# Moving small work of a two-layer encoder between VectorE, ScalarE and Pool, with warm-up matmuls and latent units spread wider

## The chip, the cores and the metric

The kernel runs on one core of one Trainium2 chip. A core has TensorE (PE) with its weight loads (PEld), VectorE (DVE), ScalarE (ACT), GpSimd (POOL) and SyncE (SP), which starts the transfers. Each engine works off its own list of instructions in the order in which the program wrote them, and waits on semaphores of the others. The metric is the time on the device in microseconds, the median of three runs. Beside it stands one execution that the hardware profiler recorded, from which all durations come.

## The reference

`x` has 512 tokens of 1024 numbers in float32, and there are two layers:

```python
for l in range(DEPTH):
    h = rms_norm(x, attn_norm_g[l])
    c_q, c_kv, k_rope, gq, gk, gv, pool_in, gate_logits = split_columns(h @ w_in[l], IN_SIZES)
    o_mla = mla_branch(c_q, c_kv, k_rope, ...)     # low-rank q and kv, 8 heads, norms of heads, rope
    o_gqa = gqa_branch(gq, gk, gv, ...)            # 8 query heads, 2 key heads, norms of heads, rope
    o_pool = pool_branch(pool_in, ...)             # centred means over 2/4/8/16 tokens, minus the token
    gates = sigmoid(gate_logits)                   # three gates of 1024 columns
    merged = sum(gates[:, :, i] * (o_i @ w_branch_i) for the three branches)
    x = x + merged @ w_out[l]
    u = depthwise_conv(rms_norm(x, ffn_norm_g[l]) @ ffn_w_up[l], ...)
    x = x + (silu(u_gate) * u_val) @ ffn_w_down[l]
```

An RMS norm multiplies a row by the inverse root of its mean square. Such inverse roots are needed for the rows before both halves of a layer, for the two latents, and for the heads of queries and keys.

## The kernel before, in words

**Products.** TensorE's numbers are rounded float32 (fp32r). To keep the accuracy, every operand is cut in two, a high part (a copy that rounds) and a low part (the rest), and a product is three matmuls (`mm3`, lines 347 to 351): high by high, high by low, low by high. The weights are cut on the chip too: `w_split` (line 301) lets ScalarE copy the high part `wh` and VectorE or Pool subtract it, which gives `wl`. Four buffers of each go round, two pieces ahead of their use. Which engine subtracts is chosen by `pick` when the program is built, after the first eight pieces of the first layer, which are VectorE's.

**Order.** The program is written by a planner that runs while the kernel is built. `Clock` keeps a modelled time; `chain` starts each step of a chain of small operations when the step before would be done, `at` starts one at a given delay, `need` and `done` keep keys that a step waits for, and `Engine` books a modelled cost for every operation. The order in which the operations fall in this model is the order of each engine's list. So a change of one operation or of its booked cost can move others. No modelled time is read in this document.

**Stages of a layer.**

1. The latents: `tok_major` multiplies token blocks of `HH`/`HL` (high and low part of `x` times its gain) with eight pieces of 384 columns, into banks acc and ST. In the first layer `norm_steps` (line 382) makes `HH` on ScalarE, `HL` on VectorE, the squares `sqt` in turn on VectorE and ScalarE, and their sum `sq` on Pool, while the eight blocks of `x` arrive.
2. `norm_finish` (line 428): TensorE sums `sq` over the partitions, `rsqrt_steps` (line 405) takes the inverse root `rt` of 8 columns in ten operations on VectorE (a first guess from the bits and three Newton steps), then `dgh` and `dgl` are set up from it, from which TensorE and ScalarE make `rbc`, the root along the other axis (`norm_rows`, line 451).
3. Four groups of pool columns, `feat_major`, 24 matmuls each, into banks AV, AV, mi and S. `pool_steps` (line 601) evacuates each as `pp`, adds shifted copies (`win`, one to four sums by group), scales the edges, subtracts the token, and cuts the result in two (`mxh`, `mxl`).
4. The latents are scaled with their root `ssc`, turned by TensorE and cut (`cth`, `ctl`).
5. Queries of the grouped attention: eight pieces of 512 into AV, AV, mi and ST, then squares (`gqs`), rope (`rp`, `gqr`) and scaling by the root `ssr` (`gq_norm`, line 712).
6. Keys and values: eight pieces of 288, and in the middle `pool_product` (line 724), which uses the query banks again. The key `gk` gets rope and root, is turned (`gk_turn`, line 780) and cut into `ka` and `kb`.
7. Two attentions of eight heads, with filler units between their steps: gate units (`gate`, 3 matmuls of 512), branch units (`branch`), and units of the second attention's queries, keys and values from the latents (`make_q`, `make_n`, `make_v`). `gates` (line 804) gives them out, one latent unit before each gate or branch unit as long as there are latent units. Gate, branch and latent units share the two acc banks. `attention` holds a table of fixed positions for its own steps among the filler.
8. The output projection, the up projection with its convolution, and the down projection, bound by TensorE alone; the next layer's `HH`, `HL` and `sq` are made beside the last one.

`tables` (line 515) multiplies the rope tables with the gains of the heads, `tabg` four times 128x256 and `tabm` four times 128x128, on VectorE, once in a layer.

In the profile most rows stand at the line of a helper: L208 is ScalarE's activation, L215 a tensor_tensor and L219 a scalar_tensor_tensor of VectorE or Pool, L223 a reduction, L227 a tensor_scalar, L340 the matmul, L344 the turn.

Of the kernel before, what the change touches and what calls it, by code (L numbers as in the profile page):

```python
# [187 lines left out]
class Engine:  # L188
# [20 lines left out]

    def _two(self, out):  # L210
        self._count(out, *((0.002145, 0.127) if self.kind == "Pool" else (0.00105, 0.07)))

    def tensor_tensor(self, out, *a):
        self._two(out)
        return self.eng.tensor_tensor(out, *a)  # L215
# [27 lines left out]
def trunk(ctx: ExitStack, tc: tile.TileContext, x, w, prm, gb, cst, out):  # L243
# [115 lines left out]
    ident = C[:, C_ID:C_ID + P]  # L359
    ones = cp.tile([P, P], F32R, tag="ones", name="ones")  # L360


# [18 lines left out]

    def norm_steps(gen, kc, g, sq, sqe=None):
        xk = XM[:, kc, :]
        hh, hl = HH[:, kc, :], HL[:, kc, :]
        t = sq if kc == 0 else slot("sqt")

        def hi():
            A.activation(hh, xk, AF.Copy, scale=g)
            if sqe is None:
                A.activation(t[:, :T], xk, AF.Square)  # L390

        def lo():
            V.scalar_tensor_tensor(hl, xk, g, f(hh), ALU.mult, ALU.subtract)
            done("H", gen, kc)

        def add():
            if sqe is not None:
                sqe.tensor_tensor(t[:, :T], xk, xk, ALU.mult)
            if kc > 0:
                G.tensor_tensor(sq[:, :T], sq[:, :T], t[:, :T], ALU.add)  # L400
            done("sq", gen, kc)

        return [hi, lo, add]

    def rsqrt_steps(a, n, key, eng=None):

        y = small("y0", [P, 64])[:, :n]
        t = small("yt", [P, 64])[:, :n]

        def newton(to):  # L410
            if eng:
                eng.tensor_tensor(t, y, a, ALU.mult)
                eng.tensor_tensor(t, t, y, ALU.mult)
# [12 lines left out]
        return [go, lambda: done(*key)]  # L426
# [47 lines left out]

    def rope_steps(dst, src, cs, sn, shape, half, eng2):

        hold = []

        def parts():
# [10 lines left out]
            if dst is not src:  # L490
                V.tensor_tensor(dst, src, cs, ALU.mult)

        def add():
            if dst is src:
                V.tensor_tensor(dst, src, cs, ALU.mult)
            V.tensor_tensor(dst, dst, hold[0], ALU.add)

        return [parts, add]

    def layer(l, sq, xsrc):  # L500
# [14 lines left out]
        def tables():  # L515
# [85 lines left out]
        def pool_steps(g, acc, tag):  # L601
# [13 lines left out]
            def window(step):  # L615
# [164 lines left out]
        def gk_turn():  # L780
# [4 lines left out]
            def hi():  # L785
                for j in range(2):
                    ka, kb = KAB[j]
                    js = slice(64 * j, 64 * j + 64)
                    A.activation(ka[0:64, :T], kT[js], AF.Copy)
                    A.activation(ka[64:128, :T], kT[js], AF.Copy)  # L790

            def lo():
# [5 lines left out]
                done("kab", l)  # L798
            chain(hi, lo)

# [3 lines left out]
        def gates(br, okey, odst, mode):  # L804
# [46 lines left out]

            extra = None
            for k, m in _order(br):
                if k in mla_make:
                    extra = mla_make[k](m)
                    continue
                work = branch(m) if k == "b" else gate(m)
                more = True
                while more:
                    if extra:  # L860
                        if next(extra, END) is END:
                            extra = None
                        yield
                    more = next(work, END) is not END
                    yield
# [26 lines left out]
        def q_out(g, b, acc):  # L892
            j = slot("mqs")

            def copies():
                copy(MQ[g][:, b].rearrange("p h f -> p (h f)"), acc[:, :384])

            def squares():
                A.activation(j[:, :384], acc[:, :384], AF.Square)
# [5 lines left out]

            chain(copies, squares, sums)

# [51 lines left out]
        def n_out(g, p, acc):  # L959
# [6 lines left out]
            def squares():  # L966
                A.activation(j[:, :T], acc, AF.Square)
# [5 lines left out]

            chain(copies, squares, sums)

# [412 lines left out]
    nc.scalar.dma_start(prms[0][:, :PRM_W0], prm[0][:, :PRM_W0])  # L1388
    warm = small("warm", [P, 1], bufs=1)
    V.memset(warm, 0.0)  # L1390
# [9 lines left out]
    for j in range(LA + 1):  # L1400
        at(4.05 + 1.27 * j, lambda j=j: w_ahead(j))
    for kc in range(KC):
# [139 lines left out]
```

## Time and profile before

| | |
|---|---|
| median of 3 runs (1677.89 to 1677.95) | 1677.89 us |
| the profiled execution | 1680.6 us |
| its span, first to last instruction | 1678.8 us |
| mean granted TensorE clock | 0.996 |
| VectorE, ScalarE, Pool busy | 57%, 46%, 53% |
| layer 0 up to the output projection, and layer 1 likewise | 0 to 372 us, 845 to 1202 us |

A row of the timeline gives the start and the length in us, the engine, the line, the operation, what it writes and reads, the shape, and in brackets how long the engine had been idle before it and which operation ended that. "x3" means three operations in a row, and the length is that from the first one's start to the last one's end. A row of the windows gives for a stretch the busy time and, in brackets, the number of instructions of PE, PEld, DVE, ACT and POOL, then the granted clock, the share of the transfer engines, and GB/s.

### The profile page before, as it was taken

The numbers are of one execution on the slowest core, as the hardware profiler recorded it, in microseconds if no ns is written. First come the engines' busy times: TensorE is split into PE (matmuls) and PEld (weight loads), VectorE is DVE, ScalarE is ACT, GpSimd is POOL, SyncE is SP. The second block draws the span as 40 slices with busy tenths as digits, with TensorE's granted clock in tenths as the row PEclk, the third lists the DMA queues.
The fourth block names the chain that finished last, engine by engine and source line by source line (L and its number), as shares of the span: only waits on it lengthen the run. The fifth ranks groups of instructions, "written<-read, shape, count | busy, mean of one in ns | idle before, by whom it ended". The sixth has DMA issues, their size and how long they took to land.

```text
span 1678.8 us, 20300 instructions
## 1 busy us (share of the span) xinstructions
PE 1650.0 (98%) x7360; PEld 1336.1 (80%) x7360; DVE 949.4 (57%) x1542; ACT 774.0 (46%) x1364; POOL 886.6 (53%) x746
## 2 busy tenths in 40 slices
PE   8989999999999999999999999999999999999999
PEld 7777777778888888888887877777788888888887
DVE  7777767753356667630157677677533666666100
ACT  5356755553444444432234577455534444444221
POOL 4432763444566666655544427643446666566543
PEclk9999999999999999999999999999999999999999
DMA  4221111113323333233232211111233222222331
GB/s 174 79 85 44 57 61 53 48 52 124 124 86 93 96 94 100 88 112 114 99 108 79 82 45 60 60 51 47 70 116 119 88 93 96 99 90 90 113 118 57
DMA packets 44596, 145.40 MB, mean 87 GB/s; under 512 B 5072, under 2 KB 6352, under 8 KB 44496
## 3 DMA queue, kind: packets, MB, share of 16 engines
q1 hardware_dynamic: 44352, 144.10, 26.0%
q8 instruction: 58, 0.95, 0.2%
q14 instruction: 42, 0.34, 0.1%
q10 hardware_dynamic: 144, 0.01, 0.0%
HBM read 139.90 MB, written 4.19 MB: 86 GB/s over the span
## 4 chain that ended last, share of the span: by engine, by line
PE 91%; issue 4%; DVE 2%; ACT 1%; POOL 1%; DMA 0%; SPq 0%; POOLq 0%; DVEq 0%; ACTq 0%
PE ps_acc L340 41%; PE ps_ST L340 23%; PE ps_AV L340 23%; PE ps_S L340 2%; PE ps_mi L340 1%; POOL wl L215 1%; PE ps_mi L344 1%; DMA XM<-x 0%; ACT qa L208 0%; ACT wh L208 0%; DVE vml L215 0%; DVE nm L223 0%; DVE gqr L215 0%; ACT ka L208 0%; DVE vmh L231 0%
## 5 line engine op out<-in xcount | busy, mean ns | idle before, releaser
L215 POOL TENSOR_TENSOR wl<-raw,wh 128x512 fp32r<-128x512 f32 (+1 forms) x514 | 679.8, 1332 | 659.2 <-ACT wh L208 548.1
L208 ACT ACTIVATE wh<-raw 128x512 fp32r<-128x512 f32 (+3 forms) x522 | 315.0, 610 | 193.0 <-PE ps_ST L340 92.6
L219 DVE SCALAR_TENSOR_TENSOR a<-u,prm,a 128x512 f32<-128x512 f32 x176 | 239.8, 1363 | 79.4 <-ACT a L208 76.0
L340 PE MATMUL ps_acc<-HH,wh 128*128 128x512 f32 x592 | 234.7, 396 | 3.2 <-DVE XM L219 3.0
L340 PE MATMUL ps_acc<-HH,wl 128*128 128x512 f32 x592 | 234.0, 395 | 1.2 <-POOL wl L215 1.2
L340 PE MATMUL ps_acc<-HL,wh 128*128 128x512 f32 x592 | 233.6, 395 | 0.0
L340 PEld LDWEIGHTS ps_acc<-HH,wh 128*128 128x128 f32 x592 | 111.5, 188 | 30.3 <-ACT wh L208 4.5
L340 PEld LDWEIGHTS ps_acc<-HH,wl 128*128 128x128 f32 x592 | 111.4, 188 | 28.5 <-POOL wl L215 2.1
L340 PEld LDWEIGHTS ps_acc<-HL,wh 128*128 128x128 f32 x592 | 111.5, 188 | 25.4
L208 ACT ACTIVATE ps_ST<-ps_ST 128x512 f32<-128x512 f32 x128 | 74.5, 582 | 120.7 <-PE ps_ST L340 120.2
L340 PE MATMUL ps_AV<-HH,wh 128*128 128x512 f32 x288 | 113.9, 396 | 0.0
L340 PE MATMUL ps_AV<-HL,wh 128*128 128x512 f32 x288 | 113.8, 395 | 0.0
L340 PE MATMUL ps_AV<-HH,wl 128*128 128x512 f32 x288 | 113.7, 395 | 0.0
L223 DVE TENSOR_REDUCE nm<-ps_S 128x1 fp32r<-128x512 f32 x128 | 87.5, 684 | 45.1 <-PE ps_S L340 44.3
L215 DVE TENSOR_TENSOR pl<-ps_ST,ph 128x512 fp32r<-128x512 f32 x128 | 87.2, 682 | 32.8 <-ACT ph L208 32.2
L215 POOL TENSOR_TENSOR al<-a,ah 128x512 fp32r<-128x512 f32 x44 | 58.3, 1326 | 84.8 <-ACT ah L208 56.6
L340 PE MATMUL ps_ST<-HH,wh 128*128 128x512 f32 x240 | 95.0, 396 | 0.0
L340 PE MATMUL ps_ST<-HL,wh 128*128 128x512 f32 x240 | 94.8, 395 | 0.0
L340 PE MATMUL ps_ST<-HH,wl 128*128 128x512 f32 x240 | 94.8, 395 | 0.0
L208 ACT ACTIVATE a<-u,prm 128x512 f32<-128x512 f32 x88 | 72.0, 818 | 31.8 <-DVE u L215 31.8
L208 ACT ACTIVATE ah<-a 128x512 fp32r<-128x512 f32 x44 | 27.8, 633 | 116.3 <-DVE u L239 110.8
L208 ACT ACTIVATE a<-a 128x512 f32<-128x512 f32 x44 | 27.9, 635 | 113.7 <-DVE u L239 113.7
(343 smaller groups left out, 3545.4 us busy)
## 6 DMA issues: line engine op xcount, KB each, us to landing
raw<-w SPq DMA_DIRECT2D x228, 512.0 KB, 3.4
raw<-w SPq DMA_DIRECT2D x13, 384.0 KB, 2.9
XM<-x SPq DMA_DIRECT2D x16, 256.0 KB, 3.8
raw<-w SPq DMA_DIRECT2D x6, 448.0 KB, 3.3
xsp<-XM SPq DMA_DIRECT2D x8, 256.0 KB, 2.0
XM<-xsp SPq DMA_DIRECT2D x8, 256.0 KB, 3.3
out<-XM SPq DMA_DIRECT2D x8, 256.0 KB, 2.3
raw<-w SPq DMA_DIRECT2D x4, 432.0 KB, 3.0
```

Source lines behind the costliest of these rows:

```text
L208: return self.eng.activation(out, in_, func, **k)
L215: return self.eng.tensor_tensor(out, *a)
L219: return self.eng.scalar_tensor_tensor(out, *a)
L223: return self.eng.tensor_reduce(out, in_, *a, **k)
L340: PE.matmul(o, lhsT=lhsT, rhs=rhs, start=start, stop=stop)
L344: PE.transpose(o, src, ident)
```

## The change

- Pool gets from VectorE: the tables of the ropes, the window sums of the two wider pool groups, the last sum of the query ropes, and the scaling of the queries by their root. VectorE gets from Pool: the seven sums of squares in the first layer's start.
- All squares at that start are made by ScalarE, later than the cuts of `x`.
- Inverse roots of 8 columns become one power with exponent -0.5 on Pool (two for the rows, one for the latents, one for the key heads, in each layer). Roots of 32 columns stay as they were.
- The second copies of the key's high part are made by VectorE from the first ones and no longer by ScalarE from PSUM; the low part is placed 1.2 us later in the planner's time.
- Copy and squares of a latent unit are issued together.
- A latent unit comes before every second gate or branch unit.
- 34 matmuls of 128x128 on a tile of ones run at the start, and their result is not used.

```diff
-        self._count(out, *((0.002145, 0.127) if self.kind == "Pool" else (0.00105, 0.07)))
+        self._count(out, *((0.14, 0.1) if ALU.pow in a else (0.002145, 0.127) if self.kind == "Pool" else (0.00105, 0.07)))
...
-            if sqe is not None:
-                sqe.tensor_tensor(t[:, :T], xk, xk, ALU.mult)
             if kc > 0:
                 G.tensor_tensor(sq[:, :T], sq[:, :T], t[:, :T], ALU.add)
...
     def rsqrt_steps(a, n, key, eng=None):
+        if n == 8:
+            return [lambda: G.tensor_tensor(a, a, bc(mhalf, [P, 8]), ALU.pow), lambda: done(*key)]
...
             if dst is not src:
-                V.tensor_tensor(dst, src, cs, ALU.mult)
+                eng2.tensor_tensor(dst, src, cs, ALU.mult)
...
-            V.tensor_tensor(dst, dst, hold[0], ALU.add)
+            (eng or eng2).tensor_tensor(dst, dst, hold[0], ALU.add)
...
-                    V.tensor_tensor(
+                    G.tensor_tensor(
                         tb[:, 256 * i:256 * i + 256].rearrange("p (b f) -> p b f", b=4),
...
-                V.tensor_tensor(
+                G.tensor_tensor(
                     tabm[:, 128 * n:128 * n + 128].rearrange("p (b f) -> p b f", b=4),
...
-            chain(([("w", KC - 1), ("H", G1, KC - 1), ("sq", G1, KC - 1)], tables), after=16.0)
+            chain(([("rt", G1)], tables), after=20.0)
...
-                V.tensor_tensor(nx[:, c0:c1], wins[-1][:, i0[0]:i0[1]], wins[-1][:, i1[0]:i1[1]], ALU.add)
+                (G if g >= 2 else V).tensor_tensor(nx[:, c0:c1], wins[-1][:, i0[0]:i0[1]], wins[-1][:, i1[0]:i1[1]],
+                                                   ALU.add)
...
-            parts, add = rope_steps(o, q, cs, sn, [P, 8, 64], 32, V)
+            parts, add = rope_steps(o, q, cs, sn, [P, 8, 64], 32, V, G)
...
-            V.tensor_tensor(o, o, bc(ssr[:, 8 * b:8 * b + 8].unsqueeze(2), [P, 8, 64]), ALU.mult)
+            G.tensor_tensor(o, o, bc(ssr[:, 8 * b:8 * b + 8].unsqueeze(2), [P, 8, 64]), ALU.mult)
...
-              *[([("gqr", l, b)], lambda b=b: gq_norm(b)) for b in range(4)])
+              *[([("gqr", l, b), ("gkn", l)], lambda b=b: gq_norm(b)) for b in range(4)])
...
-                    A.activation(ka[64:128, :T], kT[js], AF.Copy)
+                    V.tensor_copy(ka[64:128, :T], ka[0:64, :T])
...
-            chain(hi, lo)
+            chain(hi, lambda: at(1.2, lo))
...
-                    extra = mla_make[k](m)
+                    extra, tick = mla_make[k](m), 0
...
-                    if extra:
+                    if extra and tick % 2 == 0:
...
+                    tick += 1
...
-            chain(copies, squares, sums)
+            chain(copies, sums)
...
+    idle = ps("mi")
+    for _ in range(34):
+        PE.matmul(idle[:, :P], lhsT=ones, rhs=ones, start=True, stop=True)
+    free("mi")
...
+    def square(kc, t):
+        A.activation(t[:, :T], XM[:, kc, :], AF.Square)
+        done("sqt", kc)
+    def sum_up(kc, t):
+        if kc > 0:
+            V.tensor_tensor(sq[:, :T], sq[:, :T], t[:, :T], ALU.add)
+        done("sq", 0, kc)
...
-        chain(*norm_steps(0, kc, prms[0][:, PRM_AG + kc:PRM_AG + kc + 1], sq, None if kc % 2 else V),
-              after=3.4 + 1.27 * kc)
+        chain(*norm_steps(0, kc, prms[0][:, PRM_AG + kc:PRM_AG + kc + 1], None)[:2], after=3.4 + 1.27 * kc)
+        at(9.0 + 1.27 * kc, lambda kc=kc: square(kc, sqt[kc]))
+    chain(*[([("sqt", kc)], lambda kc=kc: sum_up(kc, sqt[kc])) for kc in range(KC)], after=11.0)
```

Only the query rope is given Pool for its last sum; the key rope keeps VectorE. The built lists show the moves: VectorE's loses 114 instructions (1544 to 1430), Pool's gains 41 (751 to 792), TensorE's gains 34, and SyncE's transfers keep their order. Pool's list in each layer has the eight tables between weight subtractions of the first stage, the seven window sums between the pieces 16 to 21 of the layer, the four rope sums between the pieces 27 to 31, and the four scalings after the key's root, between the pieces 37 to 40.

More of the change, by code (lines that the diff above doesn't have):

```diff
@@ L208, in activation, with _two @@
         return self.eng.activation(out, in_, func, **k)
-    def _two(self, out):
-        self._count(out, *((0.002145, 0.127) if self.kind == "Pool" else (0.00105, 0.07)))
+    def _two(self, out, *a):
+        self._count(out, *((0.14, 0.1) if ALU.pow in a else (0.002145, 0.127) if self.kind == "Pool" else (0.00105, 0.07)))
     def tensor_tensor(self, out, *a):
-        self._two(out)
+        self._two(out, *a)
         return self.eng.tensor_tensor(out, *a)
@@ L360, in trunk @@
     ones = cp.tile([P, P], F32R, tag="ones", name="ones")
+    mhalf = cp.tile([P, 1], F32, tag="mhalf", name="mhalf")
     MQ, MK = [[cp.tile([P, 4, 4, 96], F32, tag=f"{n}{g}", name=f"{n}{g}") for g in range(2)] for n in ("MQ", "MK")]
@@ L379, in split, with norm_steps @@
         return steps
-    def norm_steps(gen, kc, g, sq, sqe=None):
+    def norm_steps(gen, kc, g, sq):
         xk = XM[:, kc, :]
         hh, hl = HH[:, kc, :], HL[:, kc, :]
-        t = sq if kc == 0 else slot("sqt")
+        t = sq if kc == 0 or sq is None else slot("sqt")
         def hi():
             A.activation(hh, xk, AF.Copy, scale=g)
-            if sqe is None:
+            if sq is not None:
                 A.activation(t[:, :T], xk, AF.Square)
@@ L473, in bc, with rope_steps @@
         return ap.to_broadcast(shape)
-    def rope_steps(dst, src, cs, sn, shape, half, eng2):
+    def rope_steps(dst, src, cs, sn, shape, half, eng2, eng=None):
         hold = []
@@ L850, in branch @@
                     chain(product, add, *split(mh[:, :T], ml[:, :T], XM[:, m, :]), fin)
-            extra = None
+            extra, tick = None, 0
             for k, m in _order(br):
                 if k in mla_make:
-                    extra = mla_make[k](m)
+                    extra, tick = mla_make[k](m), 0
                     continue
@@ L896, in copies @@
                 copy(MQ[g][:, b].rearrange("p h f -> p (h f)"), acc[:, :384])
-            def squares():
                 A.activation(j[:, :384], acc[:, :384], AF.Square)
@@ L964, in copies @@
                 copy(MK[g][:, bs, :, 0:64], acc.rearrange("p (b h f) -> p b h f", b=2, h=4))
-            def squares():
                 A.activation(j[:, :T], acc, AF.Square)
@@ L972, in sums @@
                 done("ssn", l, g, p)
-            chain(copies, squares, sums)
+            chain(copies, sums)
         def k_norm(g):
@@ L1389, in trunk @@
     warm = small("warm", [P, 1], bufs=1)
+    V.memset(mhalf, -0.5)
     V.memset(warm, 0.0)
@@ L1401, in trunk @@
         at(4.05 + 1.27 * j, lambda j=j: w_ahead(j))
+    def square(kc, t):
[5 more added lines that the diff above has]
+        done("sq", 0, kc)
+    sqt = [sq] + [slot("sqt") for _ in range(1, KC)]
     for kc in range(KC):
-        chain(*norm_steps(0, kc, prms[0][:, PRM_AG + kc:PRM_AG + kc + 1], sq, None if kc % 2 else V),
-              after=3.4 + 1.27 * kc)
+        chain(*norm_steps(0, kc, prms[0][:, PRM_AG + kc:PRM_AG + kc + 1], None)[:2], after=3.4 + 1.27 * kc)
+        at(9.0 + 1.27 * kc, lambda kc=kc: square(kc, sqt[kc]))
+    chain(*[([("sqt", kc)], lambda kc=kc: sum_up(kc, sqt[kc])) for kc in range(KC)], after=11.0)
     at(30.0, lambda: V.tensor_copy(idr, ident))
```

## The prediction

> **What bounds the kernel now.** I read the engine table of the profile first, then the list of what TensorE waited for, then the granted clock in narrow windows, and last the order of each engine around every wait.
>
> ```profile
> PE 1650.0 (98%) x7360; PEld 1336.1 (80%) x7360; DVE 949.4 (57%) x1542; ACT 774.0 (46%) x1364; POOL 886.6 (53%) x746
> ```
>
> ```profile
> 372.71 63.19 PE ps_acc L340 x273
> ```
>
> TensorE is busy 98% of the span, and in the quiet parts (second row, from the chain that ended last) one 128x512 matmul starts every 63.19 / 273 = 0.231 us. No work is taken from TensorE here, so the change can only win what TensorE idles, or runs at a low clock. Both can be counted.
>
> ```profile
> PE ps_acc L340 <- ACT wh L208: 4.9, 1, 4.9
> PE ps_ST L340 <- DVE gqr L215: 4.1, 2, 2.0
> PE ps_acc L340 <- ACT mns L208: 3.0, 2, 1.5
> PE ps_acc L340 <- DVE XM L219: 3.0, 2, 2.1
> PE ps_acc L340 <- DVE wl L215: 2.0, 2, 1.8
> PE ps_acc L340 <- DVE vml L215: 1.8, 2, 0.9
> PE ps_AV L340 <- POOL wl L215: 1.7, 2, 0.9
> ...
> PE ps_acc L340 <- ACT mqs L208: 1.2, 2, 0.9
> PE ps_AV L340 <- ACT wh L208: 0.7, 1, 0.7
> ```
>
> These are TensorE's waits (total us, times, longest). The first is the wait for the first data; the other eight sum to 17.5 us.
>
> ```profile
> 14.16:17.58 3.42, 1.58 (x9) 1.25 (x8) 3.42 (x3) 1.06 (x3) 3.20 (x3) 1.00 0.90 360
> 17.58:20.99 3.41, 3.41 (x12) 3.41 (x12) 3.41 (x5) 0.53 (x1) 1.47 (x1) 0.50 0.44 178
> 21.00:24.41 3.41, 3.41 (x21) 3.41 (x21) 3.38 (x8) 0.64 (x1) 2.78 (x2) 1.00 0.00 0
> 61.95:65.36 3.41, 3.41 (x10) 2.67 (x9) 3.41 (x5) 0.00 (x0) 3.02 (x2) 0.50 0.31 83
> 116.56:119.98 3.42, 3.42 (x12) 2.80 (x10) 1.38 (x2) 2.23 (x5) 0.39 (x1) 0.50 0.46 153
> 918.69:922.10 3.41, 1.38 (x6) 0.82 (x5) 3.27 (x10) 1.64 (x3) 0.79 (x1) 1.00 0.00 0
> 922.10:925.52 3.42, 3.42 (x16) 3.41 (x15) 3.25 (x11) 1.27 (x3) 0.80 (x1) 0.50 0.14 16
> ```
>
> The second column is TensorE's busy time and, in brackets, its matmuls; after the five engines stands the granted clock. Four stretches of 3.41 us run at 0.50; the two whose predecessor is shown follow one in which TensorE was busy under half. At half clock 12 of the 384-column matmuls run instead of 21 (rows two and three): 9 x 0.175 = 1.6 us lost. At 61.95 it is 10 of the 512-column ones instead of 3.41 / 0.231 = 14.8, 1.1 us; the two mixed stretches I put at 1.4 each. So a wait of 2 us can cost 3.5.
>
> The Trainium skill, TensorE: Matmul & The Clock Gate, section "Why this matters for your kernels", asks for no idle gap over about 3 us. By that rule gaps of 2 us would leave the clock alone, and the sum below would be 5.5 us smaller, 1665. The trace does not agree, and so this has no chance of its own: 1.38 us busy in 3.41, a gap of about 2, was followed by 0.50.
>
> **The change part by part.**
>
> *Start of layer 0.* The squares leave VectorE for ScalarE, and the seven sums leave Pool for VectorE.
>
> ```profile
> 4.89 0.69 PE L340 MATMUL ps_acc<-wh,HH 128*128 128x384 f32 x1 [4.89 <-ACT wh L208]
> 12.01 7.06 POOL L215 TENSOR_TENSOR sq<-sq,sqt 128x512 f32<-128x512 f32 x4 [3.62 <-DVE sqt L215]
> 12.33 1.34 ACT L208 ACTIVATE wh<-raw 128x384 fp32r<-128x384 f32 x3
> 14.76 4.72 DVE L215 TENSOR_TENSOR wl<-raw,wh 128x384 fp32r<-128x384 f32 x3
> 28.43 0.95 PE L340 MATMUL ps_S<-ones,sq 128*128 128x2 f32 x8
> 859.87 0.34 PE L340 MATMUL ps_acc<-wl,HH 128*128 128x384 f32 x1
> 860.05 0.34 PE L340 MATMUL ps_acc<-wh,HL 128*128 128x384 f32 x1
> ```
>
> The fourth weight block's high part was there by 12.8, its low part only after 14.76, because VectorE and Pool dragged each other: 4.72 / 3 = 1.57 us a subtraction, and 7.06 / 4 = 1.77 a sum. With Pool idle there I give the low part 0.6 us and end it near 13.5. The last two rows give a 384-column matmul at full clock 0.175 us, so five blocks of 12 take 10.5 us: the row sums at 28.43 move to about 24.2, a gain of **4.2**. The 34 warm-up matmuls start near 1.2. A third of the half-clock interval of a 384-column matmul, 3.41 / 12 = 0.28 us, is about 0.1 us each, so they end near 4.9, just as the data arrives; if each cost a full 0.33 (no overlap of its weight load) they would end after 10 and leave a gain of 1.2. The clock could rise one or two stretches earlier, but the arrival of data (12.8 above) caps what that gives, at 5.2. I take the overlapped case, since the rows show weight loads overlapping.
>
> *Pooled sums to Pool.* TensorE's waits on the AV banks (1.7 and 0.7) come from ScalarE standing in order:
>
> ```profile
> 57.90 0.63 ACT L208 ACTIVATE mxh<-win 128x512 fp32r<-128x512 f32 x1 [4.87 <-DVE win L219]
> ```
>
> ScalarE idled 4.87 us for VectorE's window sums with weight copies queued behind. Seven sums a layer move to Pool at 1.29 us. In the new order they stand between weight subtractions; laid out by hand with 1.3 us an operation, from the first window at about 43 us to the last at 58, each subtraction still ends 2 us or more before its matmul. The two waits and the half-clock stretch go: **3.5**. Behind the new wait of Pool for VectorE's first window stand the weight pieces 17 to 21, with that slack.
>
> *Tables and query scalings to Pool.* TensorE waits twice 2.0 us for the ST bank, held by the fourth rope on VectorE.
>
> ```profile
> 87.84 0.75 DVE L219 SCALAR_TENSOR_TENSOR opl<-ps_AV,prm,oph 128x512 fp32r<-128x512 f32 x1 [1.34 <-ACT oph L208]
> 89.77 0.68 DVE L215 TENSOR_TENSOR gqr<-ps_ST,tabg 128x512 f32<-128x512 f32 x1
> ```
>
> In the new order this rope stands ahead of `opl` (0.7) and of the 1.34 us of idling before it, and three sums of 0.6 us or more have left: 89.77 + 0.68 = 90.45 becomes about 86.5, while TensorE asks 2.0 us ahead of 90.5. Both waits and the stretch at 922 go: 4.1 + 1.4 = **5.5**. The four sums and four scalings cost Pool 8 x 1.29 = 10.3 us a layer. The scalings wait for `gkn`, with weight pieces 38 to 41 behind them; by my layout the last scaling ends about 2 us ahead of the query transposes, and piece 40 within 0.5 us of its matmul. Eight tables cost Pool 4 x 0.74 plus four of half the size, about 5 us. In layer 1:
>
> ```profile
> 849.80 5.47 POOL L215 TENSOR_TENSOR wl<-raw,wh 128x384 fp32r<-128x384 f32 x5
> ```
>
> Three of these five (1.09 each) end at 853.1, the tables at 858.1, the eighth block's subtraction at 859.2; the matmul that needs it starts at 859.87. That is hidden by 0.7 us.
>
> *Latent units, squares and key copies.* The product that frees an accumulator stood on VectorE behind the key's low part, which waited for ScalarE:
>
> ```profile
> 110.79 2.39 ACT L208 ACTIVATE ka<-ps_mi 64x512 fp32r<-64x512 f32 x4
> 113.22 1.39 DVE L215 TENSOR_TENSOR kb<-ps_mi,ka 64x512 fp32r<-64x512 f32 x2 [3.23 <-ACT ka L208]
> ```
>
> Two of the four copies leave ScalarE (1.2 us) and the gate ahead of them is earlier. A latent unit of q (6 x 0.175 = 1.05 us) now has two gate units (2 x 0.69) instead of one between it and the next, and its copy and square stand together. Waits on XM (3.0), mqs (1.2) and the stretch at 116.56 (1.4): I take 4.5 of 5.6. Waits on mns (3.0) and vml (1.8): I take 3.5 of 4.8. Together **8.0**; 2 at the low end, 10.4 at the high.
>
> *Roots as one power.* No row shows a power on Pool.
>
> ```profile
> 862.79 0.17 DVE L227 TENSOR_SCALAR rt<-ps_S 128x8 f32<-128x8 f32 x1 [6.42 <-PE ps_S L340]
> 862.99 0.17 DVE L227 TENSOR_SCALAR y<-rt 128x8 int32<-128x8 int32 x1
> 864.80 0.17 DVE L219 SCALAR_TENSOR_TENSOR rt<-yt,y 128x8 f32<-128x8 f32 x1
> 865.89 0.69 DVE L215 TENSOR_TENSOR dgl<-C,rtl 128x512 fp32r<-128x512 f32 x1
> 868.28 0.39 PE L340 MATMUL ps_acc<-dgh,ones 128*128 128x512 f32 x1
> ```
>
> Ten operations from 862.99 to 864.97, 2.0 us, become one. TensorE comes 1.7 us after `dgl`, so a power may take 2.0 + 1.7 = 3.7 us before it costs anything. From below, the nearest rows:
>
> ```profile
> L215 POOL TENSOR_TENSOR XM<-XM,gt 128x512 f32<-128x512 f32 x16 | 20.7, 1293 | 0.6 <-DVE gt L219 0.6
> L215 POOL TENSOR_TENSOR rp<-MQ,tabm 128x256 f32<-128x256 f32 x8 | 5.8, 740 | 0.0
> L215 POOL TENSOR_TENSOR yt<-y,ssm 128x32 f32<-128x32 f32 x12 | 3.1, 254 | 3.0 <-DVE y L227 2.2
> ```
>
> A product of 32 columns takes 0.25 us; the kernel's own planner is given 1.22 us for the power. I take 1.2, hidden, and keep 10 as the other end. While a power waits or runs, weight pieces queue on Pool and the casts of the root on VectorE.
>
> *Sum.* 4.2 + 3.5 + 5.5 + 8.0 = 21.2 gained. I set 3.0 against it: 1 us a layer where piece 40 is due, and 1 for attention, whose 900 lines of changed order I cannot follow wait by wait. Net 18.2. The profiled execution took 1680.6 (span 1678.8 and 1.8 around it): 1662.4. The median of the runs is 2.7 below it: **1659.7**.
>
> **The rivals.**
>
> *Pool drags VectorE.* Against the change stands this row:
>
> ```profile
> 102.06 1.78 DVE L215 TENSOR_TENSOR gk<-gkn,tabg 128x512 f32<-128x512 f32 x1
> ```
>
> The same shape takes 0.68 when no Pool operation runs beside it (the row at 89.77). About 23 operations a layer are new on Pool. If 15 of them hold a VectorE operation for half of 1.29 us, that is 10 us a layer; with half of it on the way to a matmul, 10 us in all return: 1670. For it: the key's rope, root and scaling lie where the new scalings lie. Against it: VectorE loses about as much work there. The Trainium skill, SBUF — State Buffer, section "SBUF: two separate sides", says this as a rule: a VectorE operation with two SBUF inputs and a Pool operation take turns for a whole instruction. The rows agree.
>
> *The power is dear* (slower). It decides at four roots a layer: two of the row norms with 3.7 us of cover, the key's with about 5, the latents' with about 9. Two layers of (p - 3.7) x 2 + (p - 5) eat 18.2 at p = 7.2 us, 28 times the 0.25 of the nearest row. At 10 us it costs 2 x (6.3 x 2 + 5 + 1) = 37, and the time is 1697.
>
> *The waits only change their name.* The next releaser in each place is nearly as late and the gains shrink to the start alone: 1677.9 - 4.2 + 3.0 = 1676.7. Against it: most places have 2 us or more behind the removed wait.
>
> *Order in attention goes wrong.* The attention's places in the filler are fixed numbers, and they meet new ready times. From 18.2 us on it decides; if six of the eight heads of each kind wait 1 us more in both layers, that is 2 x 2 x 6 = 24 us: 1684. Against it: in the waits listed, attention's own operands hardly stand.
>
> **How the numbers follow.** The forecast, 1653 to 1668, has 0.62; better than that 0.05; Pool dragging VectorE, 1668 to 1674.5, 0.14; waits renamed 0.07; the dear power 0.06; attention 0.06. A measurement of this kernel tells about 0.2%, 3.4 us, from no change. Faster 0.81, same 0.07, slower 0.12. The start's and the latents' bounds (1.2 to 5.2, 2 to 10.4) lie inside the range 1651 to 1675, which holds 0.8.
>
> **What would show it.** Right: row sums near 24, no 0.50 clock after the start, no wait on ST for `gqr`, none on AV for a weight, a power near 1.2 us. Wrong: `wl` of Pool as TensorE's chief releaser between 95 and 125 or after 925, a power over 4 us, or warm-up matmuls still running at 6.

## The result and the profile after

The changed kernel takes 1662.86 us (median of 4 runs, 1662.54 to 1663.14) against 1677.89 before: a ratio of 0.991, 95% interval 0.9893 to 0.9927, 15.0 us less. The profiled execution took 1662.54 with a span of 1660.7; the span is 18.1 us shorter than that of the execution profiled before, which lay 2.7 us above its median. For one of the experiments below (eight wide warm-up matmuls) one of four executions, the profiled one, ran slow at 5776.6 us; its time and trace are not used.

The list of what TensorE waited for in the kernel after gives the releaser, the time in all, how often, and the longest:

```profile
PE ps_acc L340 <- POOL wl L215: 3.0, 2, 2.5
PE ps_mi L340 <- DVE nm L223: 1.9, 1, 1.9
PE ps_mi L1395 <- DVE ones L239: 1.1, 1, 1.1
PE ps_acc L340 <- DVE XM L219: 0.8, 3, 0.5
PE ps_ST L340 <- DVE qb L215: 0.7, 1, 0.7
PE ps_acc L340 <- DVE vml L215: 0.5, 2, 0.3
PE ps_acc L340 <- ACT mqs L208: 0.4, 1, 0.4
```

No wait for `gqr`, none on an AV bank, and little is left for the latents (`vml`, `mqs`, `XM`). What leads the list now is a weight's low part from Pool, once for 2.5 us. The table by engine on the page:

```profile
PE 1648.2 (99%) x7394; PEld 1339.3 (81%) x7394; DVE 918.7 (55%) x1428; ACT 773.2 (47%) x1366; POOL 921.5 (55%) x787
```

VectorE lost 31 us of work and Pool gained 35, yet TensorE's span fell by 18. A share of busy time would not have told that; the stages do. I cut both traces at the first matmul of each stage, found in TensorE's timeline. This gives us per stage, from one profiled execution each (that of the kernel before lay 2.7 us above its median, so its column holds some time that most of its executions do not). The last six columns are the changed kernel with one edit undone or varied, and they are used below:

| stage, us | before | after | no warm-up | unit ahead of every gate unit | Newton roots | query work on VectorE | sums on VectorE | copies undone |
|---|---|---|---|---|---|---|---|---|
| start to row sums, layer 0 | 28.43 | 26.59 | 24.26 | 26.31 | 26.64 | 26.85 | 27.41 | 26.54 |
| row sums to latent turns, 0 | 23.67 | 23.78 | 23.77 | 23.78 | 23.76 | 23.77 | 23.77 | 23.77 |
| latent turns to pooled product, 0 | 34.12 | 30.23 | 30.27 | 30.25 | 32.17 | 30.27 | 31.03 | 30.26 |
| pooled product to key turn, 0 | 22.68 | 20.40 | 20.40 | 20.40 | 20.39 | 22.70 | 20.40 | 20.40 |
| key turn to first MLA turn, 0 | 136.33 | 130.52 | 130.54 | 134.37 | 133.72 | 129.56 | 130.49 | 130.94 |
| latent turns to pooled product, 1 | 31.55 | 30.19 | 30.19 | 30.19 | 30.87 | 30.19 | 30.20 | 30.19 |
| pooled product to key turn, 1 | 24.19 | 20.39 | 20.39 | 20.38 | 20.37 | 22.68 | 20.38 | 20.38 |
| key turn to first MLA turn, 1 | 133.55 | 135.59 | 135.57 | 132.18 | 135.72 | 136.59 | 136.55 | 132.47 |

A stage that an edit doesn't touch repeats within about 0.1 us from kernel to kernel (second row), with two exceptions. At the start the moment of the clock's rise differs from run to run. In the last row half-clock stretches come and go behind waits of the same length: the granted clock of that stage shows one after the change and one without warm-up, two with the query work and two with the sums on VectorE, and none in the other four columns. In the other rows half a microsecond is legible where in the whole time it is not: the kernel before took 1677.89, 1678.37, 1678.65 and 1678.52 us in its four sets of runs, and single runs from 1675.4 to 1680.6.

Layer 1's last stage is longer than before. TensorE there, in the timeline after (start, length, and in brackets the idle time before it):

```profile
991.72 0.28 PE L340 MATMUL ps_acc<-wh,cth 128*128 128x256 f32 x1
994.47 0.46 PE L340 MATMUL ps_acc<-wl,cth 128*128 128x256 f32 x1 [2.47 <-POOL wl L215]
```

Pool's timeline shows what the weight stood behind:

```profile
989.54 0.63 POOL L215 TENSOR_TENSOR yt<-y,ssm 128x32 f32<-128x32 f32 x1 [1.99 <-DVE y L227]
...
993.49 0.25 POOL L215 TENSOR_TENSOR ssm<-yt,y 128x32 f32<-128x32 f32 x1
993.70 0.72 POOL L215 TENSOR_TENSOR wl<-raw,wh 128x256 fp32r<-128x256 f32 x1
```

The first and the last of the twelve operations of the MLA queries' root, and then the piece that TensorE wants. Pool had idled 1.99 us for the first guess `y`, which VectorE made at 989.29. Pool executes in order, so the piece, whose copy was ready, waited out a root that it has nothing to do with. The windows around it (busy time and matmuls of PE first, the granted clock behind the five engines):

```profile
991.20:994.60 3.40, 0.93 (x5) 0.50 (x4) 1.99 (x3) 2.14 (x4) 2.81 (x10) 1.00 0.00 0
994.60:998.05 3.45, 3.45 (x11) 2.86 (x12) 1.38 (x2) 1.46 (x3) 3.45 (x3) 0.51 0.50 152
```

A window with 0.93 us of work, then one at 0.51: the only stretch after the start in which TensorE still works at half clock.

### The profile page after: what moved, and what is told of

The parts are those of the page before. It is cut to its first block, busy times and chain, and to the rows that moved or that the text cites. A ratio compares the mean times of both kernels' runs of the same rounds, so it can differ in the third digit from the quotient of the medians.

```text
span 1660.7 us, 20300 instructions
## 1 busy us (share of the span) xinstructions
PE 1648.2 (99%) x7394; PEld 1339.3 (81%) x7394; DVE 918.7 (55%) x1428; ACT 773.2 (47%) x1366; POOL 921.5 (55%) x787
## 4 chain that ended last, share of the span: by engine, by line
PE 96%; DVE 2%; ACT 1%; POOL 1%; issue 0%; POOLq 0%; DVEq 0%
PE ps_acc L340 42%; PE ps_ST L340 24%; PE ps_AV L340 24%; PE ps_S L340 3%; PE ps_mi L340 2%; PE ps_mi L344 1%; PE ps_mi L1395 0%; POOL wl L215 0%; POOL MQ L215 0%; DVE nm L223 0%; DVE rp L215 0%; DVE kb L215 0%; ACT ps_ST L208 0%; DVE pl L215 0%; ACT ph L208 0%
## 5 line engine op out<-in xcount | busy, mean ns | idle before, releaser
L215 POOL TENSOR_TENSOR wl<-raw,wh 128x512 fp32r<-128x512 f32 (+3 forms) x508 | 665.5, 1319 | 601.4 <-ACT wh L208 511.4
```

## The experiments

Ratios are to the kernel before on the same chip. The changed kernel's own is 0.991.

### The warm-up

```diff
-    idle = ps("mi")
-    for _ in range(34):
-        PE.matmul(idle[:, :P], lhsT=ones, rhs=ones, start=True, stop=True)
-    free("mi")
```

> The changed kernel without the 34 warm-up matmuls. Theory A (the warm-up only holds back the first real matmul: 34 at 0.215 us, first real one at 8.42): first real matmul near 5.0, row sums near 25 against 26.59, 1661 to 1662 us. Theory B (the delay pays, since data collects meanwhile and TensorE has no half-empty window later): a half-clock stretch comes back between 14 and 21, row sums at 27 or later, 1663 to 1665 us.

```diff
-    for _ in range(34):
+    for _ in range(16):
```

> The changed kernel with 16 warm-up matmuls in place of 34 (16 x 0.215 = 3.4 us, so they end near 4.6, before the first data at 5.0). Theory A: as without any, row sums near 25, full clock from 11 to 12. Theory C (a warm-up does raise the clock, and only its length was wrong): full clock before 9, row sums near 24, 1660 us. Theory B: row sums at 27.

```diff
-    for _ in range(34):
-        PE.matmul(idle[:, :P], lhsT=ones, rhs=ones, start=True, stop=True)
+    wide = small("wide", [P, T], F32R, bufs=1)
+    V.memset(f(wide), 1.0)
+    for _ in range(8):
+        PE.matmul(idle, lhsT=ones, rhs=wide, start=True, stop=True)
```

> The changed kernel with 8 warm-up matmuls of 128x512 in place of 34 of 128x128 (8 x about 0.43 = 3.4 us, from 1.4 to 4.8). Theory D (the small ones did not count because half of their time is the weight load): full clock from 8.2 or earlier, row sums near 24, 1660 us. Theory A: as with 16 small ones, full clock not before 10.7, row sums near 25.

Measured: none 1660.44 us (0.9889, 0.9874 to 0.9904), 16 small ones 1660.13 (0.9889, 0.9873 to 0.9906), 8 wide ones 1659.77 to 1661.19 (0.9889, 0.9872 to 0.9905). TensorE's first rows in the changed kernel, and the windows around the clock's rise in it:

```profile
1.10 7.52 PE L1395 MATMUL ps_mi<-ones 128*128 128x128 f32 x34 [1.10 <-DVE ones L239]
8.42 0.63 PE L340 MATMUL ps_acc<-wh,HH 128*128 128x384 f32 x1
```

```profile
8.20:11.60 3.40, 3.40 (x12) 3.40 (x13) 2.68 (x4) 2.88 (x6) 0.00 (x0) 1.00 1.06 390
11.60:15.00 3.40, 3.40 (x22) 3.40 (x21) 2.52 (x5) 3.07 (x7) 0.00 (x0) 1.00 1.06 360
```

and without the warm-up:

```profile
5.02 0.69 PE L340 MATMUL ps_acc<-wh,HH 128*128 128x384 f32 x1 [5.02 <-ACT wh L208]
...
9.54 0.47 PE L340 MATMUL ps_acc<-wh,HH 128*128 128x384 f32 x1
9.86 0.34 PE L340 MATMUL ps_acc<-wl,HH 128*128 128x384 f32 x1
```

A warm-up matmul took (8.42 - 1.10) / 34 = 0.215 us, so 34 of them held the first real matmul back by 3.4 us. The clock didn't come sooner for it: from 8.20 to 11.60 twelve matmuls ran, the half pace, and the full pace began near 11.6; without any warm-up it began at 9.86, with 16 at 9.58. These are single executions, and the moment varies: in the seven traces here with 34 warm-up matmuls the full pace began between 11.0 and 13.5, in the two later kernels with 16 at 11.6 and 11.2. The row sums stay apart all the same, 26.31 to 27.41 with 34 against 24.15 to 24.92 with 16 or none. So theory A holds in what the warm-up does, with row sums at 24.26 and 24.15; both kernels are a little faster than the 1661 to 1662 us and the row sums near 25 that it gave. Theory B falls, since nothing ran at half clock between 14 and 21 without the delay. Of theory C the time came out, but by the clock's row not for its reason, as no warm-up at all does as well. Whether wide ones raise the clock stays open; their time is that of none. It also stays open what keeps the small ones from raising it: their size, their weight loads or their constant operand.

### The eight-column roots

```diff
-        if n == 8:
-            return [lambda: G.tensor_tensor(a, a, bc(mhalf, [P, 8]), ALU.pow), lambda: done(*key)]
```

> One part undone: the eight-column roots again as ten VectorE operations in place of one power of Pool (1.65 to 1.86 us there). My theory (the power is hidden and so is what it replaces): within 1.5 us of 1662.9. Rival (freeing VectorE of the ten operations is what keeps the key stage on time): 2 to 5 us slower, in the stretch from the pooled product to the key turn.

Measured: 1670.37 us, 0.9951 (0.9938 to 0.9963). My theory was wrong: the span grew by 7.1 us. The rival had the direction, too small, and named a stretch that did not change (20.39 and 20.37); the loss lies in the latents' stage and behind the key turn. VectorE's and ScalarE's timelines of this run, around layer 0's key:

```profile
96.37 1.26 DVE L227 TENSOR_SCALAR y<-ssr 128x8 int32<-128x8 int32 x1
...
100.08 0.17 DVE L219 SCALAR_TENSOR_TENSOR ssr<-yt,y 128x8 f32<-128x8 f32 x1
...
101.55 0.68 DVE L215 TENSOR_TENSOR gt<-ps_AV,rbc 128x512 f32<-128x512 f32 x1
```

```profile
102.27 0.64 ACT L208 ACTIVATE gt<-gt 128x512 f32<-128x512 f32 x1 [6.49 <-DVE gt L215]
102.81 0.92 ACT L208 ACTIVATE wh<-raw 128x384 fp32r<-128x384 f32 x2
```

and the same two operations with the power, in the changed kernel:

```profile
95.60 0.69 DVE L215 TENSOR_TENSOR gt<-ps_AV,rbc 128x512 f32<-128x512 f32 x1 [0.34 <-PE ps_AV L340]
```

```profile
96.33 0.63 ACT L208 ACTIVATE gt<-gt 128x512 f32<-128x512 f32 x1 [2.52 <-DVE gt L215]
96.86 0.51 ACT L208 ACTIVATE wh<-raw 128x384 fp32r<-128x384 f32 x1
```

The root itself was not late. Its ten operations, 96.37 to 100.25, stand ahead of the gate's product `gt` on VectorE; ScalarE stands in order for `gt`, with two weight copies behind; Pool waits 4.79 us for those copies; TensorE waits for Pool. Four engines pass one delay on, each in its own order. TensorE's list for the run has the end of it:

```profile
PE ps_acc L340 <- POOL wl L215: 5.6, 6, 2.5
...
PE ps_AV L340 <- POOL wl L215: 1.1, 2, 0.8
```

Between 100 and 116 us these waits are 1.9 us in all, and a half-clock stretch follows them:

```profile
107.20:110.60 3.40, 1.67 (x8) 1.14 (x9) 1.31 (x3) 0.87 (x2) 3.40 (x4) 1.00 0.48 147
110.60:114.05 3.45, 3.45 (x13) 3.16 (x12) 1.38 (x2) 1.82 (x3) 0.59 (x1) 0.51 0.53 157
```

The stage behind layer 0's key lost 3.2 us by both together. Another 1.9 lie in the latents' stage of layer 0 and 0.7 in that of layer 1; the rest is spread over stretches without a wait of their own and is not explained.

The same edit the other way round, on the kernel before: the power and its planner's price, and nothing else.

> The kernel before with one part alone: the roots of eight columns as one power on Pool. My theory now (the ten VectorE operations of the key's root, 3.8 us, stood ahead of the gate's product, ScalarE waited for that with weight copies behind it, and this is what undoing the power cost): 4 to 8 us faster than before, most of it from the pooled product on to the first MLA turn, and nothing at the start. Rival (undoing it cost so much only because the other parts had put so much on Pool): under 2 us.

Measured: 1673.80 us, 0.9972 (0.9962 to 0.9982), 4.7 us by medians and 6.6 by the spans of the two profiled executions (the one before lay 2.7 us above its median, this one 0.5). In size that is about the low end of what I expected; the place was wrong. Its stages: latent turns to pooled product 30.19 in both layers, which is all that the whole change gained there (34.12 and 31.55 before); pooled product to key turn 22.67 and 24.22, unchanged; key turn to MLA turn 134.52 in layer 0, 1.8 less, where the half-clock stretch at 116.56 is gone. So 5.3 of the 6.6 come ahead of the pooled product, and only the 1.8 can be the key's root. Of the ten operations of the latents' root the kernel before has the first and the last here:

```profile
40.65 1.26 DVE L227 TENSOR_SCALAR y<-ssc 128x8 int32<-128x8 int32 x1
...
45.62 0.17 DVE L219 SCALAR_TENSOR_TENSOR ssc<-yt,y 128x8 f32<-128x8 f32 x1
```

Behind them VectorE took up the second AV bank at 48.17; with the power alone it did so at 41.41. ScalarE's wait for the finished window is as long as before, but it ends sooner:

```profile
55.40 0.63 ACT L208 ACTIVATE mxh<-win 128x512 fp32r<-128x512 f32 x1 [4.86 <-DVE win L219]
```

It ends at 55.40 against 57.90, since the latents' root no longer stands ahead of the windows on VectorE. TensorE reaches the stage at nearly the same time (latent turns at 52.40, before 52.10), so both waits on the AV banks are gone, and with them the half-clock stretch at 61.95. And the price of the power, in the changed kernel, by form:

```profile
L215 POOL TENSOR_TENSOR rt<-rt,mhalf 128x8 f32<-128x8 f32 x4 | 6.6, 1648 | 2.2 <-DVE rt L227 2.2
L215 POOL TENSOR_TENSOR ssc<-ssc,mhalf 128x8 f32<-128x8 f32 x2 | 3.7, 1858 | 0.0
L215 POOL TENSOR_TENSOR ssr<-ssr,mhalf 128x8 f32<-128x8 f32 x2 | 3.3, 1646 | 0.2
```

### What moved to Pool, one thing at a time

```diff
-                    G.tensor_tensor(
+                    V.tensor_tensor(
                         tb[:, 256 * i:256 * i + 256].rearrange("p (b f) -> p b f", b=4),
...
-                G.tensor_tensor(
+                V.tensor_tensor(
                     tabm[:, 128 * n:128 * n + 128].rearrange("p (b f) -> p b f", b=4),
```

> One part undone: the eight tables of a layer on VectorE again, at the new place behind the roots. My theory (of the 6.1 us gained from the pooled product to the key turn the tables hold little, since they are made 60 us ahead of their use): 0 to 1.5 us slower than 1662.9. Rival (the tables delay the window sums behind them on VectorE): 2 to 4 us slower, with the loss before the pooled product.

Measured: 1663.60 us, 0.9913 (0.9899 to 0.9926). In size as my theory had it, but partly by luck. No window sum is late (30.20 and 30.19 in that stage), and the stage where my theory looked did not change (20.38 and 20.39). The edit costs where neither theory put it, in layer 0's row norms, where row sums to latent turns take 25.43 us, 1.65 more. Layer 1's last stage takes 133.84, 1.75 less, for a reason told in the last section, and so the two nearly cancel. In the row norms the diagonal now stands behind the tables on VectorE:

```profile
PE ps_acc L340 <- DVE dgh L215: 1.1, 1, 1.1
```

```diff
-                (G if g >= 2 else V).tensor_tensor(nx[:, c0:c1], wins[-1][:, i0[0]:i0[1]], wins[-1][:, i1[0]:i1[1]],
-                                                   ALU.add)
+                V.tensor_tensor(nx[:, c0:c1], wins[-1][:, i0[0]:i0[1]], wins[-1][:, i1[0]:i1[1]], ALU.add)
```

> One part undone: all window sums on VectorE again. My theory (they held the copies of the AV banks and with them a half-clock stretch): 3 to 5 us slower than 1662.9, all of it between the latent turns and the pooled product, with TensorE waiting on the AV banks again. Rival (the tables and roots that left VectorE suffice): under 1 us.

Measured: 1664.02 us, 0.9914 (0.9900 to 0.9927). The stage grew by 0.8 us in layer 0 and by nothing in layer 1: the rival's case, though the median is 1.2 us above the changed kernel's and not under 1. TensorE waits on an AV bank once, 0.6. The profiled execution also has a second half-clock stretch in layer 1's last stage (136.55 against 135.59), behind a wait of 1.9 us that the changed kernel has too.

```diff
-            parts, add = rope_steps(o, q, cs, sn, [P, 8, 64], 32, V, G)
+            parts, add = rope_steps(o, q, cs, sn, [P, 8, 64], 32, V)
...
-            G.tensor_tensor(o, o, bc(ssr[:, 8 * b:8 * b + 8].unsqueeze(2), [P, 8, 64]), ALU.mult)
+            V.tensor_tensor(o, o, bc(ssr[:, 8 * b:8 * b + 8].unsqueeze(2), [P, 8, 64]), ALU.mult)
```

> One part undone: the four last sums and four scalings of the grouped queries on VectorE again. My theory (they held the rotated query that the transposes wait for): 3 to 6 us slower than 1662.9, between the pooled product and the first query turn, with a half-clock stretch back near 110 or 915. Rival (with tables, sums and roots gone VectorE has room for them): within 1 us, or faster, since ten microseconds of work leave Pool's queue, where weight pieces stand.

Measured: 1668.28 us, 0.9935 (0.9922 to 0.9947). My theory holds, and both layers show it alike: 2.3 us from the pooled product to the key turn, and TensorE's old wait is back, without the half-clock stretch that the theory put near 110 or 915:

```profile
PE ps_ST L340 <- DVE gqr L215: 4.1, 2, 2.0
```

### The latents: spacing and copies

```diff
-                    if extra and tick % 2 == 0:
+                    if extra:
```

> One part undone: a unit of the latents again ahead of every gate unit instead of every second. My theory (the spacing is what took the waits of the latents' turns, some 4 us in layer 0, and it costs 1 to 2 us in layer 1 where later units pile up): key turn to first MLA turn 3 to 5 us longer in layer 0 and up to 3 shorter in layer 1, 1664 to 1667 us. Rival (the spacing only moves the waits; the earlier squares and key copies took them): within 1 us of 1662.9.

Measured: 1665.03 us, 0.9919 (0.9904 to 0.9934). The stages are as my theory had them, a little beyond its end in layer 1: key turn to MLA turn 3.85 us longer in layer 0, 3.41 shorter in layer 1. These nearly cancel, so they are not what makes the run 2.2 us slower. Those 2.2 lie behind the first MLA turn of both layers (616.98 us up to the next row sums against 615.99, and 604.4 to the end against 603.3), spread thin where TensorE hardly waits; their cause is open, and that the total fell into the theory's range was luck. The largest part of layer 0's loss is this wait of TensorE:

```profile
199.71 0.22 PE L340 MATMUL ps_mi<-idr,nm 128*4 128x128 f32 x1 [2.09 <-DVE nm L223]
```

```diff
-            chain(copies, sums)
+            chain(copies, squares, sums)
...
-                    V.tensor_copy(ka[64:128, :T], ka[0:64, :T])
+                    A.activation(ka[64:128, :T], kT[js], AF.Copy)
-            chain(hi, lambda: at(1.2, lo))
+            chain(hi, lo)
```

The first two lines stand for the latent queries and for the keys.

> One part undone: the copy and the square of a latent bank as two steps again, and the second key copy on ScalarE with the low parts right behind (the spacing of the latent units stays). My theory (in the 8.0 I gave to this part and the spacing, about 2 are the spacing, by the run with a unit ahead of every gate unit; the copies hold the rest): 2 to 4 us slower than 1662.9, between the key turn and the first MLA turn, with TensorE waiting for XM or mqs. Rival (the power alone made ScalarE's queue early enough): within 1 us.

Measured: 1660.50 us, 0.9894 (0.9879 to 0.9910). Both theories miss: undoing this part does not cost, and the run is nearly 2.4 us faster than the changed kernel, though the two intervals overlap. The stages say where: 0.4 us longer in layer 0, 3.1 shorter in layer 1. Pool's timeline there:

```profile
993.35 1.98 POOL L215 TENSOR_TENSOR wl<-raw,wh 128x256 fp32r<-128x256 f32 x2 [5.54 <-PE ps_S L340]
995.48 0.26 POOL L215 TENSOR_TENSOR yt<-y,ssm 128x32 f32<-128x32 f32 x1 [0.15 <-DVE y L227]
```

The weight pieces go ahead of the root, and the wait of 2.5 and the half-clock stretch behind it are gone. Two different edits, spacing and copies, each taken back, remove the same wait by another order on Pool.

### Two attempts to remove that wait

```diff
-                      *rsqrt_steps(ss[:, 0].rearrange("p g b c -> p (g b c)"), 32, ("ssmq", l), G),
+                      *rsqrt_steps(ss[:, 0].rearrange("p g b c -> p (g b c)"), 32, ("ssmq", l)),
```

> The changed kernel with 16 warm-up matmuls (1660.1 us) and the 32-column root of the MLA queries on VectorE, nine operations for Pool's twelve. My theory (a weight piece behind that root makes TensorE wait 2.6 us near 992 and then run a stretch at half clock, 1.6): 2.5 to 4.5 us faster, 1655.6 to 1657.6. Rival (the nine operations hold VectorE, on which the row maxima of attention stand, and the wait moves there): within 1 us of 1660.1 or slower.

Measured: 1660.21 us, 0.9892 (0.9878 to 0.9905), no gain over 16 warm-ups alone. The rival's time came out, and its mechanism in part. Pool's wait falls to 0.5 in all, and the guess with the nine operations, 988.89 to 991.15, holds a row maximum on VectorE:

```profile
991.81 0.22 PE L340 MATMUL ps_mi<-idr,nm 128*4 128x128 f32 x1 [1.12 <-DVE nm L223]
```

Layer 1's stage still gained 1.9 us (133.65), although a half-clock stretch (0.50 from 1021.8 to 1025.2) now follows a wait of 1.9 us for another row maximum; with 16 warm-ups alone the same wait, at nearly the same time, was followed by 1.00. Layer 0's stage lost 0.6 in the new order, and the start, with the clock's rise later in this run (11.57 against 9.58), 0.8. So part of what cancelled the gain is where the clock's windows fell.

```diff
-                    if extra and tick % 2 == 0:
+                    if extra and (l or tick % 2 == 0):
```

> The changed kernel with 16 warm-up matmuls, and latent units ahead of every second gate unit in layer 0 only, ahead of every one in layer 1. My theory (in layer 1 the spacing brings the query root and the weight piece together; without it the stretch from query turn to MLA turn is 3.4 us shorter): 1656 to 1658 us. Rival (that the stretch was shorter there came from the phase of the clock's grid alone): 1659 to 1660.5.

Measured: 1657.50 us (1657.48 to 1657.86), 0.9876 (0.9863 to 0.9890), as my theory had it; the stage takes 132.22. Pool's timeline has the pieces before the root again:

```profile
984.38 1.98 POOL L215 TENSOR_TENSOR wl<-raw,wh 128x512 fp32r<-128x512 f32 x2 [1.22 <-ACT wh L208]
986.48 0.25 POOL L215 TENSOR_TENSOR yt<-y,ssm 128x32 f32<-128x32 f32 x1
```

This is the fastest version here, about 5 us below the changed kernel.

## Why the prediction was right, and where its terms were not

The sum was 18.2 us off the profiled execution, and the spans differ by 18.1. The median fell by only 15.0: the execution profiled before lay 2.7 us above its median, and I took the same distance for the one after, which lay 0.3 below. By stages the four terms measured 1.8, 5.3, 6.1 and 3.8, 17.0 in all, against 21.2 less 3.0; the other 1.1 lie in stretches that no part aimed at. The agreement of the sum is partly luck, as its terms show: three of them are off, and what filled one was an edit that I had priced at nothing.

**The start, 4.2: 1.84 measured** (1.0 to 2.1 by the seven traces with 34 warm-up matmuls). The part about subtractions and sums was right: without the warm-up the row sums come at 24.26, the 24.2 of the text. The failed step is "about 0.1 us each, so they end near 4.9". I took a third of the interval of a 384-column matmul for the price of a warm-up of 128 columns; measured, it was 0.215, twice that. A weight load stands before each, and by its rows one lasts 0.33 us on average and overlaps its neighbours; which of the two sets the interval is not shown. The text's sign for being wrong (still running at 6) came true.

**Pooled sums, 3.5: the stage gained 3.9 and 1.4, but the sums did not do it.** The power alone gives the same 30.19 in both layers, and taking the sums back costs 0.8 and nothing. With the roots as Newton steps, the rest of the change, the sums in it, still brings the stage of layer 0 from 34.12 to 32.17. So either relief helps; the power suffices, and then little is left for the sums. I had read VectorE as late "for the window sums" and not asked what else stood ahead of them.

**Tables and query scalings, 5.5: 6.1 measured**, 2.3 and 3.8. The queries carry 2.3 a layer, and the 1.5 left in layer 1 fits the half-clock stretch at 922 in the kernel before (by size; no run isolates it). That stretch is gone in every run without the wait; of the two runs with it, the power alone has it (24.22) and the query work on VectorE does not (22.68). The tables carry nothing in this stage.

**Latents, squares and key copies, 8.0, with 3.0 set against it: 3.8 measured**, 5.8 gained in layer 0 and 2.0 lost in layer 1. In layer 0 the spacing is worth 3.85, the copies 0.4; the power has a share there too, 1.8 alone and 3.2 where it is undone, so these do not add up to 5.8. In layer 1 spacing and copies together make the collision on Pool, and either one taken back returns 3.1 to 3.4. The 3.0 set against the sum named piece 40 and attention as a whole; the loss came in attention, at 991, from a weight behind a root. With it one more of the text's signs for being wrong came true, a weight of Pool as TensorE's chief releaser after 925.

**The power, 1.2 us and nothing gained: 1.65 to 1.86, and worth 7.1 of the span where it is undone, 6.6 alone (4.7 by medians).** This is the largest error. I counted the ten operations as hidden because the root's own result had cover, 3.7 to 9 us. What mattered was what stood behind them on VectorE: behind the latents' root the windows of the pool groups (5.3 in the two layers, with the power alone), and behind the key's root the gate's product, for which ScalarE waited with weight copies behind (3.2 where the power is undone).

**The rivals.** Pool dragging VectorE was there in single rows, without ending the gain. In VectorE's timeline of the changed kernel:

```profile
986.26 1.32 DVE L227 TENSOR_SCALAR ssm<-ssm 128x32 f32<-128x32 f32 x1
```

beside this one of Pool:

```profile
986.23 1.31 POOL L215 TENSOR_TENSOR ol<-oraw,oh 128x512 fp32r<-128x512 f32 x1 [1.19 <-ACT oh L208]
```

Thirty-two columns that end with the Pool operation, 0.04 us behind it; they made the `ssm` that `y` and then the root needed, with three more operations of VectorE in between. The Trainium skill, SBUF — State Buffer, section "SBUF: two separate sides", describes the port pair as locked for a whole instruction, and the two rows agree. The dear power and an attention out of order as a whole did not come.

## What to carry to other kernels

Cost an operation that leaves an engine by what stands behind it in that engine's order, and follow it through the next engines' orders, not by whether its own result had time to spare. When several reliefs act on one queue, test each alone and each undone: here one of them sufficed, and the stage's gain belonged to another edit than the one aimed at it. A chain of small operations on the engine that also feeds the weights can hold a weight back, so look at what is queued behind its first operation, and at whether that first operation has to wait. And before a difference of 1 to 2 us is put down to an edit, look whether a half-clock stretch came or went with it.

## What the runs showed of the hardware

**Small warm-up matmuls did not raise the clock.** TensorE worked without a gap from 1.10 us to beyond 11.6 in the changed kernel, and its 384-column matmuls started 0.32 us apart until then and 0.17 apart after it; without warm-up the full pace began 4.8 us after the first matmul (5.02 to 9.86). The granted clock in the windows stands at 1.00 all through, so only the matmuls' spacing tells it. The Trainium skill, TensorE: Matmul & The Clock Gate, section "Why this matters for your kernels", asks for 4 us of continuous work to reach the full clock; without warm-up the trace comes near, but with 34 matmuls of 128x128 in fp32r it does not agree, 10.5 us against 4 (9.9 to 12.4 in the seven traces).

**Whether a wait costs a half-clock stretch depends on where it falls.** With the tables on VectorE, the same wait (2.49 us, for the same weight) was followed by full pace. The half-clock stretches of the kernel before start whole multiples of 3.413 us after one another (17.58, 61.95, 116.56, 922.10), so I count windows of that length from the clock's rise. The windows with the tables on VectorE:

```profile
992.50:995.91 3.41, 1.77 (x9) 1.08 (x7) 2.48 (x4) 2.88 (x5) 2.57 (x11) 1.00 0.00 0
995.91:999.33 3.42, 2.57 (x14) 2.17 (x15) 1.01 (x2) 0.95 (x2) 3.42 (x4) 1.00 0.45 126
```

The wait falls on two windows, with 1.77 and 2.57 us of work; in the changed kernel all of it fell into one, with 0.93. The stage took 133.84 there and 135.59 here: 1.75 us between two kernels with the same waits in that stage. How little work a window must hold is not shown: in the kernel before, a window with 1.84 us of work (58.54 to 61.95) was followed by half clock.
